# DeltaNet loop in six flows whose TensorE order is written by a planner in the source, with changed inverse and sums of squares

## Chip, cores and metric

The kernel runs on one core of a Trainium2 chip. The metric is the device time of one execution in microseconds; the median of three runs counts.

## The reference

Two encoder layers over x of 1024 tokens x 1024 channels, in f32. Layer 0 is grouped-query attention and a convolutional FFN, layer 1 a bidirectional gated DeltaNet and a convolutional FFN. The change lies in the DeltaNet, cut here to what matters:

```python
qkv, z, ab = split(h @ w_in)                      # 8 heads of q and k, 16 of v and z, 128 wide
qkv = silu(depthwise_conv_centred(qkv, conv_w, conv_b))       # 5 taps along the tokens
q = l2norm(q) * 128 ** -0.5 ; k = l2norm(k)       # each repeated for two v heads
g = -exp(a_log) * softplus(a + dt_bias) ; beta = sigmoid(b)   # per direction
# per direction, chunks of C tokens: decay from cumsum(g), L = (k*beta) k^T * decay below the diagonal
# u, w = (I + L)^-1 [v*beta, k*beta*exp(gc)]
# step: v_new = u - w state ; o = q_dec state + attn v_new ; state = state*g_last + k_dec^T v_new
o = rmsnorm(o_fwd + o_bwd, o_norm) * silu(z)
return o @ w_out
```

## The kernel before

The activations stay in SBUF transposed, channels on partitions. A dense product of f32 data is made from three matmuls of halves in fp32r (high x high, high x low, low x high): `split` (L109, L110) makes the halves, the first on ACT, the second on DVE, and `dense` (L134) issues the matmuls, 128x512 each. A product row (128 output channels, 1024 tokens) is 48 of them, in two PSUM banks of the pool `mm`, which has two such pairs; `sp` has one bank, `ip` one, `cp` two.

The loop runs over eight heads j, each a q and k row and two v and z rows, with two directions d, and each direction over eight chunks of 128 tokens:

- `gdn_in` makes the rows of a head in the order k, q, z0, z1, v0, v1. `conv5` convolves a row from PSUM: ACT writes one tap (L443), DVE adds four (L446), ACT applies the silu (L447). z goes through `gate_rows` (L526) to DRAM. The sums of squares of k and q are lane sums, 16 matmuls for each with a column of ones (L159), over squares by ACT (L480); `rstd` takes the power on GpSimd (L153). k is transposed (L521), scaled on DVE (L490) and transposed back (L493), then the grams k k^T and k q^T are made (L503). v is transposed (L521, copied by ACT at L471), and all go to DRAM in `pk`.
- `decay` (L528 to L553) makes for a head and direction the decayed grams: DMA of the gates, DVE (L541), exp on ACT (L543), products on DVE (L548, L549), halves in f16 (L551, L552).
- `inverse` inverts the unit triangular matrices of 16 chunk-heads together: on 32-blocks three series steps and three doubling levels, each adding a base through a matmul with the identity (`plus`, L589 and L590), then levels for 64 and 128, then one residual step (L668 to L678), whose result 2W + rW is summed in PSUM by a matmul with twice the identity (L676) and copied by ACT (L678).
- `chain` runs the chunks of a direction: state times k and q (L706, L707), DVE makes `r` (L710), the inverse times r (L722), ACT copies `y` (L724), kd times y (L728) updates the state on DVE (L732), pr times y (L734) gives o (L738). GpSimd makes `kd` (L699) and scales the state (L702).
- `head_out` squares o on ACT with its accumulator (L750), scales on GpSimd (L757), transposes (L764) and applies z on DVE (L765).
- When the heads are under way, the first half of the output projection (L818) follows in the same pools.

The order of all engines comes from the tile scheduler, a list scheduler that goes by priorities. `ahead(n)` raises the priority of what is issued in it; in the loop of `gdn`:

```python
with self.ahead(4):
    ah, al, prs = self.decay(j, d, *grams[j], dp)
    ws = self.inverse(d, ah, al, dp)
with self.ahead(2):
    self.chain(j, d, ws, prs, o, dp)
```

The normalisation of k and q has `ahead(2, 1100)`; products, grams, the copies of v and `head_out` have none. The scheduler thus puts the dense matmuls of the products between the dependent steps.

## Time and profile before

| | |
|---|---|
| three runs, median | 3501.07 us (3494.42 to 3502.88) |
| the profiled execution, its own time | 3503.66 us |
| its span in the profile | 3501.9 us |
| mean granted clock of TensorE | 0.983 |
| TensorE busy | 3305.3 us, 94% of the span |
| DVE, ACT, GpSimd busy | 2449.4, 1722.5, 959.9 us |

The span is the time between the first and the last instruction of the profiled execution; 1.8 us of its own time lie around it. Busy times of TensorE overlap, since a matmul begins while the one before ends, so its pace is read from the starts in the timeline. Of the span, the loop of the DeltaNet runs from about 1390 to 2664 us.

### The profile page before, as it was taken

What the parts mean: (1) busy time and instruction counts of PE and PEld (TensorE: products, weight loads), DVE (VectorE), ACT (ScalarE), POOL (GpSimd) and SP (SyncE); (2) the same over time, 40 slices, a digit from 0 to 9 for tenths busy, and PEclk for the clock granted to TensorE, in tenths of its full rate; (3) what the DMA queues carried; (4) which work ended last, traced back from release to release, by engine and by line L of the source; (5) the groups of instructions that cost most, each with busy time, mean ns of one, the idle gap of its engine ahead of it and who ended that gap; (6) DMA issues with size and microseconds to landing.
All of it is one profiled execution on the core that took longest, in us unless ns stands there. A gap on an engine that the chain in (4) does not pass through costs nothing. (4 is left out here: it accounts for less than half of the span.)

```text
span 3501.9 us, 54777 instructions
## 1 busy us (share of the span) xinstructions
PE 3305.3 (94%) x20042; PEld 2651.2 (76%) x20042; DVE 2449.4 (70%) x4133; ACT 1722.5 (49%) x3042; POOL 959.9 (27%) x1122
## 2 busy tenths in 40 slices
PE   7999999899999998999999999999898989999998
PEld 6877878677778786777777777777676867777776
DVE  5325886887777866777767677776763878777685
ACT  4224664544544454555555555556542544444443
POOL 1111230444442002122223233222231154444100
PEclk9999999999999999999999999999999989999999
DMA  3331116333324642333242333324255733322653
GB/s 125 105 103 61 33 33 198 114 103 112 103 100 152 213 132 81 100 98 113 85 135 88 114 110 108 104 88 138 84 179 170 231 105 105 109 94 99 201 163 112
DMA packets 249806, 411.23 MB, mean 117 GB/s; under 512 B 25536, under 2 KB 76096, under 8 KB 249536
## 3 DMA queue, kind: packets, MB, share of 16 engines
q1 hardware_dynamic: 249536, 407.72, 37.0%
q8 instruction: 158, 2.59, 0.3%
q14 instruction: 112, 0.92, 0.1%
HBM read 294.77 MB, written 107.61 MB: 115 GB/s over the span
## 5 line engine op out<-in xcount | busy, mean ns | idle before, releaser
L134 PE MATMUL mm<-base,wh 128*128 128x512 f32 x1248 | 480.3, 412 | 12.5 <-DVE r L818 7.4
L109 ACT CAST wh<-w_raw 128x512 fp32r<-128x512 f32 x275 | 169.8, 619 | 310.3 <-PE mm L134 210.2
L110 DVE TENSOR_TENSOR wl<-w_raw,wh 128x512 fp32r<-128x512 f32 x275 | 194.2, 709 | 147.4 <-ACT wh L109 132.7
L134 PE MATMUL mm<-yh,wh 128*128 128x512 f32 x736 | 286.2, 417 | 3.4 <-ACT yh L109 1.5
L134 PE MATMUL mm<-yl,wh 128*128 128x512 f32 x736 | 285.3, 416 | 0.8 <-DVE yl L110 0.5
L134 PE MATMUL mm<-yh,wl 128*128 128x512 f32 x736 | 282.4, 412 | 1.0 <-DVE wl L110 1.0
L153 POOL TENSOR_TENSOR rs<-rs,power 128x8 f32<-128x8 f32 (+3 forms) x30 | 60.9, 2029 | 810.2 <-DVE rs L152 810.2
L134 PEld LDWEIGHTS mm<-base,wh 128*128 128x128 f32 x1248 | 237.5, 190 | 55.9 <-issue 11.9
L134 PE MATMUL mm<-base,wl 128*128 128x512 f32 x624 | 257.3, 412 | 0.0
L699 POOL TENSOR_SCALAR kd<-c,yds 128x128 f32<-128x128 f32 x224 | 95.1, 436 | 560.7 <-PE cp L728 426.9
L109 ACT CAST wh<-s 128x512 fp32r<-128x512 f32 x216 | 134.1, 621 | 222.1 <-PE sp L134 108.8
L109 ACT CAST wh<-a 128x512 fp32r<-128x512 f32 x164 | 101.7, 621 | 261.6 <-PE mm L134 126.6
L134 PE MATMUL sp<-base,wh 128*128 128x512 f32 (+1 forms) x672 | 210.1, 370 | 1.5 <-DVE ub L995 0.9
L446 DVE SCALAR_TENSOR_TENSOR t<-mm,gdn_cw,t 128x1023 f32<-128x1023 f32 (+1 forms) x128 | 163.0, 1275 | 8.0 <-ACT t L443 6.8
L134 PEld LDWEIGHTS mm<-yh,wh 128*128 128x128 f32 x736 | 140.3, 192 | 28.3 <-ACT yh L109 3.2
L110 DVE TENSOR_TENSOR wl<-s,wh 128x512 fp32r<-128x512 f32 x174 | 144.9, 834 | 23.4 <-ACT wh L109 23.0
L134 PEld LDWEIGHTS mm<-yl,wh 128*128 128x128 f32 x736 | 139.9, 190 | 28.0 <-DVE yl L110 2.4
L134 PEld LDWEIGHTS mm<-yh,wl 128*128 128x128 f32 x736 | 140.3, 191 | 25.6 <-DVE wl L110 1.7
L134 PE MATMUL sp<-base,wl 128*128 128x512 f32 (+1 forms) x432 | 157.2, 364 | 1.6 <-DVE wl L110 1.6
L976 POOL TENSOR_TENSOR s<-a,a 128x512 f32<-128x512 f32 x80 | 105.8, 1323 | 158.4 <-DVE s L976 99.6
L134 PEld LDWEIGHTS sp<-base,wh 128*128 128x128 f32 x672 | 126.4, 188 | 24.2 <-ACT wh L109 2.0
L1054 POOL TENSOR_TENSOR t<-t,t 128x512 f32<-128x512 f32 x66 | 102.6, 1555 | 126.4 <-DVE t L1032 124.5
(536 smaller groups left out, 9510.4 us busy)
## 6 DMA issues: line engine op xcount, KB each, us to landing
a<-in_ffn_up_dram SPq DMA_DIRECT2D x160, 256.0 KB, 3.0
c<-pk SPq DMA_DIRECT2D x128, 320.0 KB, 3.0
w_raw<-in_gdn_in_dram SPq DMA_DIRECT2D x100, 256.0 KB, 3.0
g_t<-t SPq DMA_DIRECT2D x88, 256.0 KB, 2.0
raw<-g_t SPq DMA_DIRECT2D x88, 256.0 KB, 2.7
w_raw<-in_gdn_out_dram SPq DMA_DIRECT2D x68, 256.0 KB, 3.9
g<-t SPq DMA_DIRECT2D x66, 256.0 KB, 2.1
raw<-g SPq DMA_DIRECT2D x66, 256.0 KB, 2.9
```

The costliest lines, as they stand in the source:

```text
L109: self.nc.scalar.copy(out=hi, in_=src)
L110: (engine or self.nc.vector).tensor_tensor(out=lo, in0=src, in1=hi.bitcast(F32), op=ALU.subtract)
L134: self.nc.tensor.matmul(acc if one else acc[:, hs], lhsT=a, rhs=y[:, hs], start=(first and not onto and k + t == 0), stop=(last and k == n ...
L153: nc.gpsimd.tensor_tensor(out=r, in0=v, in1=self.power[:, :w], op=ALU.pow)
L446: nc.vector.scalar_tensor_tensor(out=o, in0=a, scalar=c[:, i:i + 1], in1=o, op0=ALU.mult, op1=ALU.add)
L699: nc.gpsimd.tensor_scalar(out=kd[:, e], in0=kn, scalar1=col(self.yds, e), scalar2=1.0, op0=ALU.mult, op1=ALU.mult)
L976: e.tensor_tensor(out=s[i], in0=x, in1=z, op=op)
L1054: sub = lambda out, x, z: nc.gpsimd.tensor_tensor(out=out, in0=x, in1=z, op=ALU.subtract)
```

## The change

The loop over heads becomes six flows, written as generators: `chains`, `inverses`, `prepare` (transposes, normalisation, grams, copies of v), `decays`, `heads_out` and `products`; the first half of the output projection becomes the end of `products` (`first_out`). A flow yields after some TensorE work the time of that work and the time until its result is there, both as numbers in the source, or the name of a mark that it waits for. `Weave.run` goes on with the first flow, in the order above, that is ready on its clock. TensorE keeps the order in which the instructions are issued (`manual_schedule`); the other engines are ordered by the scheduler, with the flows' priorities 5, 4, 3, 3, 1, 0.

Rows are made in the order k, q, v0, v1, z0, z1; a convolved row counts as ready 8 us after its product. The weights are fetched and split one half row ahead, at priority 1. For the sums of squares, k is copied transposed (ACT), squared by ACT with its accumulator in pieces of 128x128, and scaled by GpSimd in such pieces; q is transposed for that alone. The inverse has one first step and four levels in place of three and three; the identity lies on the diagonal of its operands, so that the matmuls with the identity go; 2W + rW is made by one DVE instruction from PSUM. Some memsets go, the pools `w` and `pr` have eight buffers in place of six, and a chain step writes kd times y into the bank of the state's product.

The order on TensorE, near the end of the loop, between the steps of a chain: from the state times q (`st,c`, 128x256) to the inverse times r (`r,w`) and on to `y,kd`. `mm<-` are dense matmuls. Before:

```order
L707 MATMUL cp<-st,c 128x256
L134 MATMUL mm<-yl,wh 128x512
L134 MATMUL mm<-base_27770,wl 128x512
L134 MATMUL mm<-yh,wl 128x512
L722 MATMUL cp<-r_27543,w 128x128 x2
L134 MATMUL mm<-base_27773,wh 128x512
L134 MATMUL mm<-yh,wh 128x512
L134 MATMUL mm<-base_27773,wh 128x512
L728 MATMUL cp<-y,kd 128x128 x2
```

After the change:

```order
L804 MATMUL cp<-st,c 128x256
L489 MATMUL mm<-base_11445,wl 128x512
L489 MATMUL mm<-yh,wl 128x512
L489 MATMUL mm<-base_11448,wh 128x512
L489 MATMUL mm<-yh,wh 128x512
L489 MATMUL mm<-base_11448,wh 128x512
L489 MATMUL mm<-yl,wh 128x512
L822 MATMUL cp<-r_19835,w 128x128 x2
```

Three dense matmuls stood on each of the two stretches of before. Now six stand on the first, and six more follow up to `y,kd`.

The order on DVE, between the four taps (L446) of a convolved row. Before, a v1 row (L110 splits weights, L753 belongs to `head_out`):

```order
L446 SCALAR_TENSOR_TENSOR t_18779<-mm_18718,gdn_cw_11735,t_18779 128x1022
L446 SCALAR_TENSOR_TENSOR t_18779<-mm_18718,gdn_cw_11735,t_18779 128x1023
L110 TENSOR_TENSOR wl_20343<-w_raw_20341,wh_20342 128x512
L446 SCALAR_TENSOR_TENSOR t_18779<-mm_18718,gdn_cw_11735,t_18779 128x1023
L753 TENSOR_TENSOR ss_20228<-ss_20228,rq_16444 128x8
L110 TENSOR_TENSOR wl_20349<-w_raw_20347,wh_20348 128x512
L446 SCALAR_TENSOR_TENSOR t_18779<-mm_18718,gdn_cw_11735,t_18779 128x1022
```

After, the k row of head 2 up to its third tap (L756 is 2W + rW, L838 adds to o, L595 and L606 belong to `decay`, L871 is z times o):

```order
L446 SCALAR_TENSOR_TENSOR t_14767<-mm_14269,gdn_cw_11730,t_14767 128x1022
L756 SCALAR_TENSOR_TENSOR w_14788<-w0_11722,ip_14783 128x512
L838 TENSOR_TENSOR o_13195<-cp_14762,o_13195 128x256
L446 SCALAR_TENSOR_TENSOR t_14767<-mm_14269,gdn_cw_11730,t_14767 128x1023
L606 TENSOR_TENSOR al_14475<-at_14483,ah_14474 128x512
L595 SCALAR_TENSOR_TENSOR pr_14488<-pr_14488,ebias_11850,maskneg_11724 128x128 x2
L756 SCALAR_TENSOR_TENSOR w_14825<-w0_11722,ip_14820 128x512
L595 SCALAR_TENSOR_TENSOR pr_14488<-pr_14488,ebias_11850,maskneg_11724 128x128 x2
L871 SCALAR_TENSOR_TENSOR z_14807<-sp_14809,gdn_gain_11732,z_14807 128x512
L446 SCALAR_TENSOR_TENSOR t_14767<-mm_14269,gdn_cw_11730,t_14767 128x1023
```

Three other instructions stood between the four taps; now nine stand between the first three taps, and after the third nine more (L602, L756, L603, L672 four times, L606, L858) come ahead of the fourth.

The diff, cut to its core:

```diff
@@ -447,53 +447,96 @@
-    def gdn_in(self, j, ys, tmp, dp, begun=None):
+    def products(self, ys, tmp, begun):
+        nc, w, cw = self.nc, self.ap["gdn_in"], self.cw5
+        rows = [(j, n, i) for j in range(8) for n, i in (("k", 8 + j), ("q", j), ("v0", 16 + 2 * j), ("v1", 17 + 2 * j),
+                                                        ("z0", 32 + 2 * j), ("z1", 33 + 2 * j))]
...
+        for p, (j, name, i) in enumerate(rows):
+            if p < 2:
+                acc = begun[p]
+            else:
+                acc = self.big()
+                for h in range(2):
...
+                    for step in self.steps(acc, split[2 * p - 4 + h], ys[4 * h:4 * h + 4], HALVES, h == 0, h == 1):
+                        yield step
+            if name[0] == "z":
+                self.gate_rows(2 * j + int(name[1]), acc, tmp)
+            else:
+                self.rows[j, name] = self.conv5(acc, cw[:, i], tmp)
+                self.weave.mark((name, j), 8.0)
...
+    def steps(self, acc, w, ys, halves, first, last):
...
+                yield 0.23 * len(halves), 0.0
...
+    def prepare(self, tmp, dp):
...
+        for j in range(8):
...
+            def sums(t, tot):
+                for n in range(4):
+                    sq = dp.tile([P, P], F32, name="sq", bufs=1)
+                    nc.scalar.activation(out=sq, in_=t[:, n * P:(n + 1) * P], func=AF.Square, accum_out=tot[:, n:n + 1])
+            yield "k", j
+            kT = self.rows[j, "k"]
+            kn = []
             for h, hs in enumerate(HALVES):
...
-        with self.ahead(2, 1100):
-            tot = self.bank()
-            for i in range(2):
-                for h, hs in enumerate(HALVES):
-                    sq = tmp.tile([P, H2], F32, name="h", bufs=2)
-                    nc.scalar.activation(out=sq, in_=kq[i][:, hs], func=AF.Square)
-                    self.lane_sums(tot[:, i * NC + 4 * h:i * NC + 4 * h + 4], sq)
-            r = self.rstd(tot[:, :2 * NC], 1, dp)
...
+                t = tmp.tile([P, H2], F32, name="h", bufs=2)
+                nc.scalar.copy(out=t, in_=self.transposed(kT[:, hs]))
+                sums(t, ss[0][:, 4 * h:4 * h + 4])
+                kn.append(t)
+                yield 0.44, 1.2
+            r = self.rstd(ss[0], 1, dp)
             for h, hs in enumerate(HALVES):
-                pt = self.transposed(kT[:, hs])
-                kn = tmp.tile([P, H2], F32, name="h", bufs=2)
-                nc.vector.tensor_tensor(out=chunks(kn), in0=chunks(pt), op=ALU.mult,
-                                        in1=r[:, 4 * h:4 * h + 4].unsqueeze(2).broadcast_to([P, 4, P]))
-                put(2, kn, slice(4 * h, 4 * h + 4))
-                nc.scalar.copy(out=kT[:, hs], in_=self.transposed(kn))
+                for n in range(4):
+                    t = kn[h][:, n * P:(n + 1) * P]
+                    nc.gpsimd.tensor_scalar(out=t, in0=t, scalar1=r[:, 4 * h + n:4 * h + n + 1], scalar2=1.0,
+                                            op0=ALU.mult, op1=ALU.mult)
+                put(2, kn[h], slice(4 * h, 4 * h + 4))
+            yield 0.0, 9.0
+            for h, hs in enumerate(HALVES):
+                nc.scalar.copy(out=kT[:, hs], in_=self.transposed(kn[h]))
+                yield 0.44, 1.5
             put(0, kT)
+            yield "q", j
+            qT = self.rows[j, "q"]
             put(1, qT)
-            kks, qks = {}, {}
+            if j > 0:
+                yield "decay", 2 * j - 1
+            kks, qks = self.grams[j] = {}, {}
             for i in (1, 0):
                 kks[i], qks[i] = (dp.tile([P, H2], F32, name=n, bufs=3) for n in ("kks", "qks"))
...
+                    yield 0.9, 1.2
+            self.weave.mark(("gram", j))
+            for h, hs in enumerate(HALVES):
+                sums(self.transposed(qT[:, hs]), ss[1][:, 4 * h:4 * h + 4])
+                yield 0.44, 2.8
+            r = self.rstd(ss[1], 1, dp)
...
+    def decays(self, dp):
+        for n in range(16):
+            if n % 2 == 0:
+                yield "gram", n // 2
+            if n > 1:
+                yield "half", n - 2
+            self.decayed[n] = self.decay(n // 2, n % 2, *self.grams[n // 2], dp)
+            self.weave.mark(("decay", n), 14.0)
+            yield 0.0, 0.0
...
-        def plus(acc, l, r, base):
-            for m in range(16):
-                nc.tensor.matmul(acc[:, m], lhsT=l[:, m], rhs=r[:, m], start=(m == 0), stop=False)
-            nc.tensor.matmul(flat(acc), lhsT=self.ident16, rhs=base, start=False, stop=True)
...
-                nc.vector.tensor_copy(out=ax[q, hs, q], in_=ah[h][q, :, q])
-            nc.vector.tensor_tensor(out=bx[:, hs], in0=ah[h], in1=every(self.mask4)[:, hs], op=ALU.mult)
-        id_all = every(self.id32)
-        for k in range(3):
-            acc = packed()
-            plus(acc, bx, tp, id_all)
+                nc.vector.tensor_tensor(out=t0[q, hs, q], in0=ah[h][q, :, q], in1=every(self.id32)[q, hs], op=ALU.add)
+            nc.vector.tensor_tensor(out=w0[:, hs], in0=t0[:, hs], in1=every(self.mask2)[:, hs], op=ALU.mult)
+        def evacuated(acc):
             tp = small("tp")
             nc.scalar.copy(out=flat(tp), in_=flat(acc))
+            return tp
...
+        acc = packed()
+        mms(acc, w0, every(self.id32))
...
+        for lv in range(4):
+            if lv:
+                wk = dp.tile([P, 16, 32], F16, name="wk", bufs=1)
+                nc.vector.transpose(out=flat(wk), in_=flat(tp))
+                for q in Q32:
+                    nc.vector.tensor_copy(out=w0[q, :, q], in_=wk[q])
             acc = packed()
-            mms(acc, ax, tp)
+            mms(acc, t0, tp)
+            yield 0.45, 3.2 if lv else 1.4
             x = small("x")
             nc.vector.tensor_tensor(out=x, in0=acc, in1=every(self.lvl[:, d, lv]), op=ALU.mult)
             acc = packed()
-            plus(acc, bx, x, flat(tp))
-            tp = small("tp")
-            nc.scalar.copy(out=flat(tp), in_=flat(acc))
+            mms(acc, w0, x)
+            tp = evacuated(acc)
+            yield 0.45, 1.2
...
+            yield 0.67, 1.2
             acc = self.ip.tile([P, 4, P], F32, name="ip")
             for m in ms:
-                nc.tensor.matmul(acc[:, m % 4], lhsT=r[:, m % 4], rhs=w0[:, m], start=(m % 4 == 0), stop=False)
-            nc.tensor.matmul(flat(acc), lhsT=self.twice16, rhs=flat(w0[:, hs]), start=False, stop=True)
-            ws[h] = dp.tile([P, 4, P], F32, name="w", bufs=6)
+                nc.tensor.matmul(acc[:, m % 4], lhsT=r[:, m % 4], rhs=w0[:, m], start=True, stop=True)
+            ws[h] = dp.tile([P, 4, P], F32, name="w", bufs=8)
+            nc.vector.scalar_tensor_tensor(out=flat(ws[h]), in0=flat(w0[:, hs]), scalar=2.0, in1=flat(acc), op0=ALU.mult,
+                                           op1=ALU.add)
+            yield 0.23, 1.2
+    def chains(self, dp):
+        for n in range(16):
+            j, d = n // 2, n % 2
+            yield "inverse", n
+            if d == 0:
+                yield "rows", j
+                self.outs[j] = [dp.tile([P, 4, 2, P], F32, name="o", bufs=3) for _ in range(2)]
+            ws, prs = self.solved.pop(n)
+            for step in self.chain(n, ws, prs, self.outs[j], dp):
+                yield step
+            self.weave.mark(("chain", n), 1.0)
...
+            if t == 4:
+                self.weave.mark(("half", n0))
+                if d == 0 and j:
+                    yield "head", j - 1
...
+                cc = a[:, 0]
+                yield 0.86, 1.0
             else:
                 r = v
+                cc = self.cp.tile([P, 2, P], F32, name="cp")
...
             nc.scalar.copy(out=y, in_=b[:, 0])
+            yield 0.45, 0.95
             if t < NC - 1:
-                cc = self.cp.tile([P, 2, P], F32, name="cp")
...
+    def heads_out(self, dp):
...
+        for j in range(8):
+            od = [self.dram.tile([P, S], F32, name=f"od{2 * j + e}") for e in range(2)]
+            for i in (1, 0):
+                yield ("half" if i else "chain"), 2 * j + 1
...
+                yield 0.0, 16.0
+                for e in range(2):
...
+                    yield 0.44, 1.5
+            self.od += od
+            self.weave.mark(("head", j))
...
-            grams = {0: self.gdn_in(0, ys, tmp, dp, begun)}
-            for j in range(8):
-                if j < 7:
-                    grams[j + 1] = self.gdn_in(j + 1, ys, tmp, dp)
-                if j == 6:
...
-                for d in range(2):
-                    with self.ahead(4):
-                        ah, al, prs = self.decay(j, d, *grams[j], dp)
-                        ws = self.inverse(d, ah, al, dp)
-                    with self.ahead(2):
-                        self.chain(j, d, ws, prs, o, dp)
-                self.head_out(j, o, dp)
-            os = self.split_rows(self.od[:8], oy, [slice(0, S)], lambda: tmp.tile([P, S], F32, name="t"))
...
+            def first_out():
+                yps.close()
+                oy.append(left.enter_context(tc.tile_pool(reuse_waits="tile", name="oy", bufs=KT)))
+                st.append(left.enter_context(tc.tile_pool(reuse_waits="tile", name="st", bufs=1)))
+                yield "head", 3
+                os = self.split_rows(self.od[:8], oy[0], [slice(0, S)], lambda: tmp.tile([P, S], F32, name="t"))
+                yield 0.0, 6.0
...
+            self.first_out = first_out
+            self.weave = Weave(self)
+            for flow, ahead in ((self.chains(dp), 5), (self.inverses(dp), 4), (self.prepare(tmp, dp), 3), (self.decays(dp), 3),
+                                (self.heads_out(dp), 1), (self.products(ys, tmp, begun), 0)):
+                self.weave.add(flow, ahead)
+            with tc.manual_schedule(engines={mybir.EngineType.PE}):
+                self.weave.run()
...
+class Weave:
+    def __init__(self, trunk):
+        self.t, self.flows, self.marks, self.now = trunk, [], {}, 0.0
+    def add(self, flow, ahead):
+        self.flows.append([flow, ahead, 0.0, None])
+    def mark(self, name, after=0.0):
+        self.marks[name] = self.now + after
+    def ready(self, f):
+        if f[3] is None:
+            return f[2]
+        return max(f[2], self.marks[f[3]]) if f[3] in self.marks else float("inf")
+    def run(self):
+        while self.flows:
+            f = next((f for f in self.flows if self.ready(f) <= self.now), None)
+            if f is None:
+                self.now = min(map(self.ready, self.flows))
+                assert self.now < float("inf")
+                continue
+            f[3] = None
+            with self.t.ahead(f[1]):
+                y = next(f[0], None)
+            if y is None:
+                self.flows.remove(f)
+            elif isinstance(y[0], str):
+                f[3] = y
+            else:
+                self.now += y[0]
+                f[2] = self.now + y[1]
```

## Rows read from the trace of the kernel before

**Rows 1.** Windows, loop stage: us; busy of PE, PEld, DVE, ACT, POOL; clock, DMA, GB/s.

```profile
1390.00:2664.00 1274.00, 1209.71 (x10297) 948.03 (x10296) 891.12 (x2015) 685.15 (x1370) 360.83 (x687) 0.99 0.37 111
```

**Rows 2.** Timeline of PE: start us, duration us, engine, line, instructions.

```profile
1911.09 0.38 PE L670 MATMUL ip<-t,nident 128*128 128x512 f16 x1
1911.12 0.58 PE L134 MATMUL mm<-yh,wl 128*128 128x512 f32 x1
1911.54 0.39 PE L134 MATMUL mm<-base,wh 128*128 128x512 f32 x1
1911.77 0.40 PE L134 MATMUL mm<-yh,wh 128*128 128x512 f32 x1
...
1917.57 0.60 PE L764 MATMUL sp<-ident,o 128*128 128x128 f32 x4
1917.93 0.48 PE L134 MATMUL mm<-yh,wh 128*128 128x512 f32 x1
1918.24 0.39 PE L134 MATMUL mm<-base,wh 128*128 128x512 f32 x1
...
2102.01 0.61 PE L734 MATMUL cp<-y,pr 128*128 128x128 f32 x4
2102.46 1.84 PE L159 MATMUL sp<-ones,h 128*128 128x1 f32 x16
```

**Rows 3.** Waits, loop stage: engine, line <- releaser: us in total, times, longest us.

```profile
PEld cp L722 <- DVE r L710: 34.0, 59, 2.2
...
PEld cp L706 <- DVE st L732: 23.3, 37, 1.5
...
PE cp L722 <- DVE r L710: 18.5, 12, 1.9
...
PEld L675 <- ACT r L672: 13.6, 46, 1.1
...
PEld L589 <- DVE bx L605: 9.9, 16, 1.1
...
PEld sp L764 <- POOL o L757: 7.7, 8, 2.6
...
PEld sp L521 <- ACT t L447: 5.5, 10, 1.9
```

**Rows 4.** Groups of DVE by form, loop stage: xcount | busy us, mean ns | idle before.

```profile
L446 DVE SCALAR_TENSOR_TENSOR t<-mm,gdn_cw,t 128x1023 f32<-128x1023 f32 x60 | 76.7, 1278 | 0.9
L541 DVE SCALAR_TENSOR_TENSOR pr<-pr,ebias,maskneg 128x128 f32<-128x128 f32 x256 | 76.7, 360 | 37.6 <-DMA pr<-grow 36.5
...
L548 DVE TENSOR_TENSOR at<-pr,kks 128x512 f32<-128x512 f32 x64 | 44.9, 702 | 11.2 <-ACT pr L543 10.5
...
L765 DVE SCALAR_TENSOR_TENSOR z<-sp,gdn_gain,z 128x512 f32<-128x512 f32 x32 | 23.9, 747 | 35.4 <-PE sp L764 23.6 <-DMA z<-zd 11.1 <-DVE yl L110 0.6
```

**Rows 5.** Groups of ACT by form, loop stage.

```profile
L750 ACT ACTIVATE sq<-o 128x128 f32<-128x128 f32 x128 | 39.9, 312 | 16.4 <-DVE o L738 13.8
...
L443 ACT ACTIVATE t<-mm,gdn_cw 128x1024 f32<-128x1024 f32 x30 | 36.2, 1206 | 1.0 <-PE mm L134 1.0
...
L447 ACT ACTIVATE t<-t 128x1024 f32<-128x1024 f32 x30 | 31.8, 1060 | 7.1 <-DVE t L446 7.0
...
L447 ACT ACT_TABLE_LOAD x15 | 19.2, 1283 | 0.3
```

**Rows 6.** A slower stretch: timeline of PE, then windows (columns as in rows 1).

```profile
2464.13 0.82 PE L722 MATMUL cp<-r,w 128*128 128x128 f32 x4 [1.88 <-DVE r L710]
...
2464.70:2468.10 3.40, 3.40 (x21) 2.85 (x20) 1.24 (x4) 0.37 (x1) 2.20 (x6) 0.50 0.55 173
```

**Rows 7.** Groups of POOL by form, loop stage, then the durations at L699.

```profile
L757 POOL TENSOR_SCALAR o<-o,ro 128x128 f32<-128x128 f32 x128 | 58.8, 481 | 5.5 <-DVE ro L755 5.5
...
L153 POOL TENSOR_TENSOR ro<-ro,power 128x8 f32<-128x8 f32 x16 | 26.8, 1673 | 241.0 <-DVE ro L152 241.0
...
L699 POOL TENSOR_SCALAR kd<-c,yds x224: 367/376/1242, 1459.4 to 2634.8; 128x128 f32<-128x128 f32 x112
```

More of the change, by code (lines that the diff above doesn't have):

```diff
@@ new lines, in steps @@
+    def steps(self, acc, w, ys, halves, first, last):
+        n = len(ys)
+        for k, ((hi, lo), (yh, yl)) in enumerate(zip(w, ys)):
+            for t, (a, y) in enumerate(((hi, yh), (hi, yl), (lo, yh))):
+                for hs in halves:
+                    self.nc.tensor.matmul(acc[:, hs] if len(halves) > 1 else acc, lhsT=a, rhs=y[:, hs],
+                                          start=(first and k + t == 0), stop=(last and k == n - 1 and t == 2))
+                yield 0.23 * len(halves), 0.0
@@ L660, in inverse @@
             nc.scalar.copy(out=w0[a, hs, b], in_=acc[a])
-        ws = {}
+            yield 0.26, 1.8
+        if n > 1:
+            yield "chain", n - 2
         for h in (range(4) if d == 0 else range(3, -1, -1)):
@@ new lines, in gdn @@
+            x = [self.dram.tile([P, S], F32, name=f"x{m}") for m in range(KT)]
+            self.first_out = first_out
[5 more added lines that the diff above has]
+                self.weave.run()
@@ L1352, in upper @@
         return ((row // b) % 2 == 0) & (row // b == col // b - 1)
[L1354 removed]
+    lv = np.stack([np.stack([m(b) | (row == col) for b in (2, 4, 8, 16)], 1) for m in (lower, upper)], 1)
     a["lvl"] = np.ascontiguousarray(lv.astype(f))
```

191 lines of the change are left out of this document (95 added, 96 removed).

## The prediction

> **What bounds the kernel now.** First the busy time by stage, because the change touches only the loop of the DeltaNet layer: from 1390 to 2664 us TensorE is busy 1209.71 of 1274.00 us and no other engine is above 891.12 [rows 1]. So what counts is TensorE's work and what makes it wait. Second, the pace of that work, from one start to the next in TensorE's timeline, because the records overlap [rows 2]. From 1911.54 to 1911.77 a dense 128x512 takes 0.23 us. From 1911.09 to 1911.54 a 128x512 in f16 and a dense one take 0.45, so the f16 one 0.22. Sixteen lane sums take 1.84, 0.115 each. From 1917.57 to 1918.24 four transposes and a dense one take 0.67, so 0.11 for a transpose. From 2102.01 to 2102.46 two f32 128x128 of the chain (four records) take 0.45. Third, TensorE's waits [rows 3]: each is small (at most 2.6 us). The largest are those of the chain for `r` and for the state `st`, which DVE makes. Convolved rows are hardly waited for: ten waits of the transposes' loads at L521, 5.5 us in the whole loop.
>
> **The change, part by part.** TensorE's instructions first; all of them lie on the path, since TensorE is the bound.
>
> A. Removed: 96 matmuls of 128x512 with the identity (six in each of 16 inverses) and 64 with twice the identity, 160 x 0.22 = 35 us; 256 lane sums, 256 x 0.115 = 29 us. Added: 64 transposes of q, 64 x 0.11 = 7 us. The small 128x32 matmuls stay 2304. Sum **-57 us**, from paces alone.
>
> B. The order of the chain. Before, three dense matmuls (0.69 us) stand between a step that makes the operand of the next and that next step; now six (1.38 us) do on both middle stretches, and four after `kd`. The weight loads waited 34.0 + 23.3 = 57 us for `r` and `st`, the matmuls themselves 18.5 for `r` [rows 3]. The 59 waits of L722 have a mean of 0.58 us, under the 0.69 that is added, the longest 2.2, above it. Bounds: 0 (DVE's queue is ordered by priorities as before and may deliver `r` as much later) and -57. I take **-35**, three fifths, nearer to the mean than to the longest.
>
> C. The inverse: four dense matmuls (0.9 us) before, six (1.34 us) now. The waits for `r` at L675 and `bx` were 13.6 + 9.9 = 23.5 us with means of 0.3 and 0.6 [rows 3]. Bounds 0 and -24; **-14**. D. The heads' outputs: 7.7 us at L764 for GpSimd's scaling [rows 3], now put 16 us behind it; bounds 0 and -8, **-5**.
>
> E. The convolved rows, where the change could lose. A row is TensorE's product, ACT's first tap (1.206 us), four taps on DVE (1.278 each, 5.1 in all) and ACT's silu (1.060, with a table load of 1.283 where another table was in use) [rows 4, 5]. Before, the readers of k, q, v0 and v1 came 46.8, 34.2, 21.9 and 12.9 us of TensorE's work after the product, counted in the order at the paces above. Now the plan puts them 8 us behind the product, and the count gives 7.7 to 14.1, mean 9.7, for the 28 rows of heads 1 to 7. And DVE, whose order the scheduler still makes with products last, has other work between the taps: 5.1 to 18.1 us from first to last tap, mean 10.3. An example is the k row shown from DVE's order (head 2). Between its four taps stand four wide instructions that read PSUM (0.747, as L765), four from SBUF (0.70, as L548) and ten narrow ones (0.36, as L541) [rows 4]: 3.0 + 2.8 + 3.6 = 9.4, with the taps 14.5; with first tap and silu 16.8 us. On TensorE there stand 23 dense matmuls (5.3), 36 of 128x128 in f16 (2.0 at a quarter of 0.22 each), three 128x512 (0.7), eight transposes (0.9), and of the chain two 128x256 and four 128x128 in f32, as much as eight 128x128 at 0.225, so 1.8: 10.7 us. It is 6 us short. The same count over the 28 rows leaves 20 short, by 113 us in sum (4 us for the order before). Below, the bound is 4: the plan's 8 us hold only if DVE leaves the taps together. Above, it is 113. The windows also hold chain and inverse steps that wait for DVE themselves, and while TensorE waits for one row DVE works off what stood before the next, so neither end is likely; no row is near either, and I take the middle, **+55**.
>
> F. The clock. At 2464.13 L722 had waited 1.88 us; from 2464.70 to 2468.10 the granted clock is 0.50, the level of 1.2 GHz [rows 6]. Such a stretch of 3.4 us costs half, 1.7 us. Twenty waits for rows of 55/20 = 2.75 us would be twenty more such stretches (34 us) if each were one wait without a break; bounds 0 and +34, I take six, **+10**.
>
> G. The start. With v ahead of z the third product is convolved too, and its bank is free only after 1.206 + 5.1 us, not after a plain evacuation, once: **+6**.
>
> Costed at nothing, with their cover. The 64 evacuations by twice-and-add on DVE (0.747 each, 48 us) and k's way over GpSimd (64 scalings for 16 DVE products) bring DVE to some 940 us of 1230: covered as long as TensorE's planned distances hold, and what they cost inside the taps is in E. ACT's squares (128 x 0.312 more for k and q [rows 5], each with a read of its accumulator, against 32 wide ones), 16 more copies and 12 more table loads of 1.283 go to an engine that is busy 685 of 1274 us [rows 1]; the loads ahead of the silu are in E. Fewer memsets free GpSimd. k's normalised form has 10.4 to 12.2 us of TensorE's work as cover; it needs 8 squares (2.5), the power on GpSimd (1.673) and 8 scalings (3.85) [rows 5, 7], 8 us, if nothing else is in the queues.
>
> A rule speaks against that last move. The scalings of the heads' outputs take 481 ns in the mean, those of L699 376 in the median and up to 1242 [rows 7]: GpSimd is sometimes held up. The Trainium skill ("SBUF — State Buffer", section "Who interferes with whom") says why: the two engines share a port pair as an exclusive lock, and a VectorE instruction with two SBUF inputs blocks a GpSimd one that reads SBUF for its whole length. By that rule, with such an instruction ahead of each scaling, the maximum would be the normal case and the sum -16 instead of -40 (rival 4); the trace agrees that it occurs, not that it is normal, as the mean of 481 shows.
>
> **The sum.** -57 - 35 - 14 - 5 + 55 + 10 + 6 = -40 us against the profiled execution of 3503.66 us, whose span is 3501.9: 3463.7. That execution is 2.6 us above the median of the runs, so I give **3461 us** for the median. 0.3% (10.5 us) is about what a measurement of this kernel can tell from no change.
>
> **The rivals.**
> 1. *The rows come late in full* (slower). TensorE stands at the first transpose of 20 of 28 rows, in all 113 us, and the clock falls after more of them (+20): -57 - 54 + 113 + 20 + 6 = +28, so 3529, and 3543 with half a microsecond more per row. For it: products have the lowest priority on DVE, and the count itself. Against it: in the trace before, DVE is 30% idle in the loop. It decides from waits of about 4 us per row over 28 rows. Chance 0.22.
> 2. *The rows are in time* (much faster): E at 4, F at 0: -57 - 54 + 4 + 6 = -101, so 3400; with B to D at their bounds 3365. For it: before, 60 such taps of each shape went by with 5.5 us of wait. Against it: there the cover was 1.3 to 4.8 times as long. Chance 0.17.
> 3. *The two cancel* (no change): rows at 95 us, so 3501. Chance 0.11. That the plan is not kept gives the same: TensorE's order is fixed, but the waits of B to D may only move to whatever engine feeds it, since DVE's order is not planned; with those terms at 0 and the rows at 40, the sum is zero.
> 4. *k's normalised form is late*. If each scaling takes GpSimd's 1242 ns, eight of them are 9.9 us and the way is 14 us against a cover of 11: 3 us for each of 8 heads, +24, so 3485. For it: that maximum; against it: the mean of 481 in the same kind of instruction. (The rule of the Trainium skill above is this rival's reason.) Chance 0.05.
>
> **The numbers.** The forecast has 0.45, with its terms between 3420 and 3490. Faster by over 0.3%: 0.45 + 0.17 + 0.05 = 0.67; within 0.3%: 0.11; slower: 0.22. The range 3392 to 3538 leaves out the far end of rivals 1 and 2, a tenth each.
>
> **What the profile would show.** A: the lines of lane sums and of identity matmuls are gone, and TensorE's matmuls in the loop take some 57 us less at the same paces. B and C: the waits for `r` and `st` fall from 57 to about 20 us. E: in the waits, the transposes and the squares' readers wait for ACT's silu, about 2 us in each row. If these waits are above 100 us in sum, rival 1 is right; if under 10, rival 2. F: stretches at a clock of 0.50 follow the transposes' waits. Rival 4 shows as waits of the second transposes of k for GpSimd. The prediction is wrong in its ground if TensorE's waits lie elsewhere, for instance on weights whose split comes late on DVE.

## The result, and the profile after

The changed kernel takes 3637.77 us (3634.67 to 3643.63), the kernel before 3501.03: a ratio of 1.0396 [1.0377, 1.0415], 137 us slower where 40 less were forecast. The profiled execution took 3643.63 us.

The page of the kernel after, first lines:

```profile
span 3641.8 us, 54329 instructions
## 1 busy us (share of the span) xinstructions
PE 3274.0 (90%) x19690; PEld 2671.0 (73%) x19690; DVE 2478.4 (68%) x4199; ACT 1735.5 (48%) x3209; POOL 925.0 (25%) x1111
...
PEclk9999999999999998999999988998989999999999
```

TensorE is busy 31 us less than before and stands still 171 us more (span less busy time). The windows from the first tap of the layer's first convolution to the last addition of the output's first half, of before and after (columns as in [rows 1]):

```profile
1362.10:2711.40 1349.30, 1270.52 (x10570) 995.45 (x10569) 927.79 (x2067) 711.32 (x1407) 363.85 (x688) 0.99 0.38 113
```

```profile
1359.20:2855.70 1496.50, 1243.92 (x10253) 1017.88 (x10252) 965.08 (x2141) 728.58 (x1581) 336.76 (x685) 0.91 0.34 101
```

The whole loss lies in this stretch: it is 147 us longer, where the spans differ by 140. The waits in it, after (columns as in [rows 3]; what was L521 is L575, L722 is L822, L706 is L803, L675 is L754, L589 is L659, L764 is L870):

```profile
PEld sp L575 <- ACT t L447: 178.6, 21, 14.3
PE sp L575 <- ACT t L447: 172.3, 21, 14.2
...
PEld cp L803 <- DVE st L832: 18.8, 17, 2.7
...
PE mm L489 <- DVE t L446: 16.0, 2, 11.1
...
PEld L754 <- ACT r L750: 14.3, 22, 3.3
...
PEld L659 <- DVE w L673: 11.2, 15, 2.9
...
PE sp L870 <- ACT h L566: 2.8, 5, 0.8
```

The first two rows are the result (the same waits, once of the weight load and once of the matmul): TensorE stood 21 times, 8.2 us in the mean, in front of the transposes of a convolved row, where before ten waits made 5.5 us [rows 3]. The loads' wait for `r` at L822 has fallen from 34.0 to 0.7 us and that for `st` from 23.3 to 18.8.

The longest of the 21 is v0 of head 3. Its way through ACT, DVE and TensorE (timelines: start, duration, engine, instruction, in brackets the idle time before):

```profile
1887.27 1.20 ACT L443 ACTIVATE t<-mm,gdn_cw 128x1024 f32<-128x1024 f32 x1
...
1908.92 1.06 ACT L447 ACTIVATE t<-t 128x1024 f32<-128x1024 f32 x1 [5.08 <-DVE t L446]
```

```profile
1888.49 0.35 DVE L595 SCALAR_TENSOR_TENSOR pr<-pr,ebias,maskneg 128x128 f32<-128x128 f32 x1
1888.75 0.69 DVE L602 TENSOR_TENSOR at<-pr,kks 128x512 f32<-128x512 f32 x1
...
1897.25 0.69 DVE L606 TENSOR_TENSOR al<-at,ah 128x512 f16<-128x512 f32 x1
1897.86 0.68 DVE L673 TENSOR_TENSOR w<-t,mask 128x1024 f16<-128x1024 f16 x1
...
1901.88 1.27 DVE L446 SCALAR_TENSOR_TENSOR t<-mm,gdn_cw,t 128x1022 f32<-128x1022 f32 x1
...
1904.35 1.27 DVE L446 SCALAR_TENSOR_TENSOR t<-mm,gdn_cw,t 128x1023 f32<-128x1023 f32 x1
...
1906.29 2.59 DVE L446 SCALAR_TENSOR_TENSOR t<-mm,gdn_cw,t 128x1023 f32<-128x1023 f32 x2
```

```profile
1895.26 0.61 PE L834 MATMUL cp<-y,pr 128*128 128x128 f32 x4
1910.03 1.11 PE L575 MATMUL sp<-ident,t 128*128 128x128 f32 x4 [14.16 <-ACT t L447]
```

ACT has the first tap done at 1888.5, but DVE's first tap starts at 1901.88: for 13 us DVE works without a break on the decay, the inverse, the chain and others, which have a higher priority. Then four more instructions stand between the taps, and the silu ends at 1909.98. The plan counted with 8 us from the product; it took 23.

This row had the longest wait, but no row kept to 8 us. From the start of ACT's first tap to the end of the silu (starts and ends in the timelines) the 28 rows of heads 1 to 7 took 16.0 us in the mean. In the kernel before the same way took 13.9 us, where 12.9 to 46.8 us of TensorE's work stood behind the product to cover it: the trace of before already had a latency well above the 8 us of the plan.

The granted clock around that wait (windows, columns as in [rows 1]):

```profile
1900.60:1914.30 13.70, 4.28 (x15) 3.60 (x15) 8.92 (x17) 3.54 (x4) 4.46 (x9) 0.50 0.17 43
```

The granted clock was 0.50, the lower of its two levels, in the later part of the wait and for 4 us behind it.

A table by stretch helps to compare the runs. For each profiled execution the time between the first convolution's first tap and the last addition of the output's first half is divided: *work* is the count of recorded matmuls times the median pace of their form in the kernel before at the full clock; what a matmul takes beyond that is *clock*, up to one more pace, in stretches granted 0.50, and *wait* for the rest (the waits of weight loads among it). It is an estimate by the rows' paces, good to some us. Each row is one execution, up to 8 us from its kernel's median; that of before took 3503.66 us, while the medians of this kernel in the sessions of the experiments are 3493 to 3499. So differences to the first row are good to some 10 us.

| kernel | window | work | clock | wait |
|---|---|---|---|---|
| before | 1349 | 1180 | 13 | 156 |
| after | 1497 | 1132 | 59 | 305 |
| after, convolutions first | 1386 | 1131 | 41 | 214 |
| after, convolutions first, no fixed order | 1368 | 1135 | 39 | 194 |
| before, all of the change's arithmetic | 1313 | 1126 | 22 | 164 |
| before, lean inverse (sum on TensorE), squares on ACT | 1297 | 1140 | 14 | 143 |
| before, lean inverse alone | 1359 | 1148 | 40 | 171 |
| before, lean inverse (sum on TensorE) alone | 1378 | 1162 | 42 | 174 |
| before, squares on ACT alone | 1333 | 1160 | 15 | 158 |
| before, 160 more wide matmuls | 1375 | 1215 | 16 | 143 |

After against before: 48 us less work, 46 more of clock, 149 more of waits.

### The profile page after: what moved, and what is told of

It reads as the page before. It is cut to its first block, busy times and chain, and to the rows that moved or that the text cites. A ratio compares the mean times of both kernels' runs of the same rounds, so it can differ in the third digit from the quotient of the medians.

```text
span 3641.8 us, 54329 instructions
## 1 busy us (share of the span) xinstructions
PE 3274.0 (90%) x19690; PEld 2671.0 (73%) x19690; DVE 2478.4 (68%) x4199; ACT 1735.5 (48%) x3209; POOL 925.0 (25%) x1111
## 5 line engine op out<-in xcount | busy, mean ns | idle before, releaser
L489 PE MATMUL mm<-base,wh 128*128 128x512 f32 x864 | 386.9, 448 | 18.4 <-DVE t L446 16.0
L110 DVE TENSOR_TENSOR wl<-w_raw,wh 128x512 fp32r<-128x512 f32 x271 | 192.7, 713 | 207.6 <-ACT wh L109 183.9
L153 POOL TENSOR_TENSOR rs<-rs,power 128x8 f32<-128x8 f32 (+2 forms) x38 | 66.6, 1752 | 863.1 <-DVE rs L152 863.1
L575 PE MATMUL sp<-ident,t 128*128 128x128 f32 x256 | 56.2, 360 | 172.9 <-ACT t L447 172.3
L489 PEld LDWEIGHTS mm<-base,wh 128*128 128x128 f32 x864 | 168.7, 195 | 43.7 <-DVE t L446 11.3
L489 PE MATMUL mm<-base,wl 128*128 128x512 f32 x432 | 197.5, 457 | 0.0
L575 PEld LDWEIGHTS sp<-ident,t 128*128 128x128 f32 x256 | 41.0, 186 | 184.6 <-ACT t L447 178.6
L489 PE MATMUL mm<-yh,wl 128*128 128x512 f32 x432 | 175.2, 406 | 0.0
L489 PE MATMUL mm<-yl,wh 128*128 128x512 f32 x432 | 173.3, 401 | 0.9 <-DVE yl L110 0.9
L489 PE MATMUL mm<-yh,wh 128*128 128x512 f32 x432 | 174.1, 403 | 0.0
L446 DVE SCALAR_TENSOR_TENSOR t<-mm,gdn_cw,t 128x1023 f32<-128x1023 f32 (+1 forms) x128 | 163.0, 1276 | 7.7 <-ACT t L443 6.6
L110 DVE TENSOR_TENSOR wl<-s,wh 128x512 fp32r<-128x512 f32 x174 | 145.1, 835 | 24.7 <-ACT wh L109 24.2
L1395 POOL TENSOR_SCALAR p<-p,m 128x1024 f32<-128x1024 f32 x60 | 68.2, 1138 | 233.7 <-DVE m L1394 171.0
```

The costliest lines, as they stand in the source:

```text
L110: (engine or self.nc.vector).tensor_tensor(out=lo, in0=src, in1=hi.bitcast(F32), op=ALU.subtract)
L153: nc.gpsimd.tensor_tensor(out=r, in0=v, in1=self.power[:, :w], op=ALU.pow)
L446: nc.vector.scalar_tensor_tensor(out=o, in0=a, scalar=c[:, i:i + 1], in1=o, op0=ALU.mult, op1=ALU.add)
L489: self.nc.tensor.matmul(acc[:, hs] if len(halves) > 1 else acc, lhsT=a, rhs=y[:, hs], start=(first and k + t == 0), stop=(last and k == n ...
L575: self.nc.tensor.transpose(out=pt[:, n * P:(n + 1) * P], in_=t[:, n * P:(n + 1) * P], identity=self.ident)
L1395: nc.gpsimd.tensor_scalar(out=p, in0=p, scalar1=m[:, 3:4], scalar2=1.0, op0=ALU.mult, op1=ALU.mult)
```

## Experiments

Times are medians; ratios are to the kernel before in the same session, with their interval. The kernel before itself had medians from 3493 to 3501 in the sessions, so a difference between runs of two sessions is given by the times and, where it matters, by the ratios.

**Convolutions first on ACT and DVE.** `ahead(6)` is above the priority of every flow.

```diff
-                self.rows[j, name] = self.conv5(acc, cw[:, i], tmp)
+                with self.ahead(6):
+                    self.rows[j, name] = self.conv5(acc, cw[:, i], tmp)
```

> The changed kernel with the convolutions' instructions at the highest priority on ACT and DVE; TensorE's order is the same. Theory (the rows come late because DVE puts the taps behind its other work): TensorE's waits for the silu at L576 fall from 180 us to under 30, the 11 us wait at the start goes, the clock recovers to about 0.98, and the time falls by 150 to 200 us, to 3440 to 3490, below the kernel before. Rival (DVE has no room left: what is taken from the taps is given back by r, st and the inverse): the waits move to the chain and the inverse, and the time stays above 3560.

Measured 3529.88 us, 1.0093 [1.0076, 1.0110], between the two ranges. TensorE's order is that of the change, so 108 of the 137 us (106 by the ratios) came from when ACT and DVE do the convolutions. The way from ACT's first tap to the end of the silu fell from 16.0 to 9.7 us in the mean. The waits now (of this kernel, whose lines stand one further):

```profile
PE sp L871 <- POOL o L863: 38.8, 20, 11.8
...
PE ip L660 <- DVE w L674: 25.2, 18, 4.0
PE cp L823 <- DVE r L808: 17.9, 27, 1.0
...
PEld sp L576 <- ACT t L447: 2.7, 2, 1.9
```

The wait for the silu fell from 179 to 3 us. But the rival has its part too: GpSimd's scaling, the inverse's first operand and `r` are now late, with the taps ahead of them on DVE, and the kernel stays above the one before.

**A later mark for the rows.**

```diff
-                self.weave.mark((name, j), 8.0)
+                self.weave.mark((name, j), 12.0)
```

> The changed kernel with one number changed: a convolved row counts as ready 12 us behind its product in place of 8. Theory (rows late on DVE): cover grows by 4 us for 28 rows, most of it against waits of 8 us in the mean, so 60 to 100 us less, 3540 to 3580. Rival (the waits follow the row wherever it is placed, since DVE's order moves along): within 30 us of the change, 3610 to 3650.

Measured 3600.11 us, 1.0299 [1.0284, 1.0314]: 38 us less (34 by the ratios), between the two ranges and nearer to the rival. The waits for the silu fell only from 172 to 132 us:

```profile
PE sp L575 <- ACT t L447: 132.2, 17, 15.3
```

So 4 us more for each of 28 rows gave 40 us. The rows moved along in part: their mean way rose from 16.0 to 18.1 us.

**No fixed order on TensorE.**

```diff
-            with tc.manual_schedule(engines={mybir.EngineType.PE}):
-                self.weave.run()
+            self.weave.run()
```

> The changed kernel without the fixed order on TensorE: the scheduler orders TensorE too, with the flows' priorities, work and buffers as in the change. Theory (the loss lies in the planned distances against DVE's order): the scheduler gives the readers of rows more distance, the waits for the silu fall under 60 us and the time to about 3450 to 3530. Rival (the loss lies in the added DVE, ACT and GpSimd work): it stays above 3580.

Measured 3525.23 us, 1.0081 [1.0066, 1.0096], within the theory's range. The scheduler keeps the rows in time, and 113 us of the loss go (110 by the ratios); the kernel is still 0.8% above before.

```profile
PEld sp L575 <- ACT t L447: 2.4, 6, 0.6
```

The rows themselves are no faster here: their mean way is 19.5 us, against 16.0 in the change. So the loss comes from rows and readers that stand too close for DVE's order: more distance, as here, and earlier taps, as with the convolutions first, each take most of it away.

**The leaner inverse alone**, in the kernel before: its `inverse` and `delta_buffers` are replaced by those of the change, without the yields.

```diff
-            plus(acc, bx, x, flat(tp))
+            mms(acc, w0, x)
...
-            nc.tensor.matmul(flat(acc), lhsT=self.twice16, rhs=flat(w0[:, hs]), start=False, stop=True)
-            nc.scalar.copy(out=ws[h], in_=acc)
+            nc.vector.scalar_tensor_tensor(out=flat(ws[h]), in0=flat(w0[:, hs]), scalar=2.0, in1=flat(acc), op0=ALU.mult,
+                                           op1=ALU.add)
```

> The kernel before with the leaner inverse alone (no matmuls with the identity or twice the identity, 2W + rW on DVE, one first step and four levels). Theory: TensorE's work falls by 160 x 0.22 = 35 us and nothing new is waited for, so 3460 to 3475 (25 to 40 us less than before). Rival (DVE's 48 us more make r and st late): no gain or a loss, 3495 to 3530.

Measured 3499.44 us, 1.0014 [1.0003, 1.0024]: no gain, in the rival's range. In the table 32 us of work are gone, and 27 of clock and 15 of waits have come.

**More work on TensorE in the same place**, the mirror of it.

```diff
-            nc.tensor.matmul(flat(acc), lhsT=self.ident16, rhs=base, start=False, stop=True)
+            for k in range(2):
+                nc.tensor.matmul(flat(acc), lhsT=self.half16, rhs=base, start=False, stop=(k == 1))
...
-            nc.tensor.matmul(flat(acc), lhsT=self.twice16, rhs=flat(w0[:, hs]), start=False, stop=True)
+            for k in range(2):
+                nc.tensor.matmul(flat(acc), lhsT=self.ident16, rhs=flat(w0[:, hs]), start=False, stop=(k == 1))
```

> The kernel before with each matmul with the identity done twice with half the identity, and that with twice the identity done as two with the identity: 160 more matmuls of 128x512 in f16, 35 us of TensorE's work, in the place where the change takes 160 away; nothing else. Theory (what a wide matmul adds there is partly given back by waits and by the clock, which fell where the leaner inverse left small matmuls alone): less than half of it is seen, 3495 to 3512, and the time at a clock of 0.50 in the loop falls below the 38 us of before. Rival (TensorE's work is the bound at full price): 3525 to 3535.

Measured 3530.41 us, 1.0118 [1.0101, 1.0135]: 38 us more for 35 us of work (26 in the table, whose execution was the fastest of this kernel's). The rival is right: what is added to TensorE here costs its full price, and the pace in term A holds. So what the leaner inverse saved was lost elsewhere.

**The leaner inverse with its sum on TensorE** (the matmul with twice the identity and ACT's copy stay; the rest as in the leaner inverse alone):

```diff
-            plus(acc, bx, x, flat(tp))
+            mms(acc, w0, x)
```

> The kernel before with the leaner inverse but 2W + rW as before, summed on TensorE by twice the identity and copied by ACT: TensorE loses 96 x 0.22 = 21 us, DVE gains nothing. Theory (in the leaner inverse alone the saving went into DVE's 48 us more and their waits): 3470 to 3480, 15 to 21 us less than before. Rival (it went into the clock, which falls after stretches of small matmuls that the wide ones no longer break up): within 8 us of before, and the time at a clock of 0.50 in the loop stays near 110 us, against 38 before.

Measured 3526.42 us, 1.0099 [1.0082, 1.0116]: slower by 34 us with 21 us less work, outside both ranges. It is not DVE's load, which is near that of before. The rival's mechanism is there: the table has 29 us more of clock, and 18 of waits. A stretch of its timeline of TensorE, and the window that follows:

```profile
1650.69 0.95 PE L159 MATMUL sp<-ones,h 128*128 128x1 f32 x8
1651.50 0.47 PE L134 MATMUL mm<-base,wh 128*128 128x512 f32 x1
1651.91 0.88 PE L632 MATMUL ip<-tp,ah 32*32 32x32 f16 x32
1652.72 0.71 PE L729 MATMUL cp<-y,pr 128*128 128x128 f32 x4
1653.27 0.95 PE L159 MATMUL sp<-ones,h 128*128 128x1 f32 x8
```

```profile
1654.20:1661.00 6.80, 6.80 (x55) 4.81 (x55) 3.55 (x10) 2.58 (x5) 2.92 (x1) 0.50 0.41 157
```

TensorE did not wait there at all. It ran 32 matmuls of 32x32 and 16 of one column (lane sums) with few wide ones between, and then the granted clock was 0.50 for 6.8 us. Nine of the 21 stretches at 0.50 in the window come right behind such 32x32 matmuls of the inverse; of the ten of before none does. In three of the nine no wait stands ahead, and there lane sums stand beside the 32x32 matmuls; in the other six TensorE had also waited, about 1 to 1.7 us, so there the two can't be told apart.

**Sums of squares by ACT and k's scaling by GpSimd alone**, in the kernel before:

```diff
-                    nc.scalar.activation(out=sq, in_=kq[i][:, hs], func=AF.Square)
-                    self.lane_sums(tot[:, i * NC + 4 * h:i * NC + 4 * h + 4], sq)
+                nc.scalar.copy(out=t, in_=self.transposed(kT[:, hs]))
+                sums(t, ss[0][:, 4 * h:4 * h + 4])
...
+                    nc.gpsimd.tensor_scalar(out=t, in0=t, scalar1=r[:, 4 * h + n:4 * h + n + 1], scalar2=1.0,
+                                            op0=ALU.mult, op1=ALU.mult)
```

> The kernel before with the sums of squares by ACT's accumulator, k's scaling by GpSimd and the transposes of q, as in the change, and nothing else of it; the scheduler orders all engines. TensorE's work falls by 22 us (256 lane sums at 0.115 less 64 transposes at 0.11). Theory (saved work is given back as in the leaner inverse alone, where 32 us less work met 27 us of clock and 15 of waits): within 10 us of before, 3485 to 3505. Rival (it pays in full, since lane sums keep TensorE's array nearly idle and their going helps the clock): 3465 to 3480.

Measured 3487.93 us, 0.9991 [0.9979, 1.0002]: no difference that can be told, as the theory had it, for 22 us less of term A's work. The clock is no better without the lane sums, 15 us against 13 in the table. (The profiled execution was 16 us shorter in the window than that of before; the other runs do not bear that out.)

**Both parts**: the leaner inverse with its sum on TensorE, and the squares, in the kernel before (the two edits above together).

> The kernel before with the parts that take work from TensorE and put little on DVE: the inverse without the matmuls with the identity, and the sums of squares by ACT with k's scaling on GpSimd. TensorE's work falls by 21 + 22 = 43 us. Theory (the parts are sound, the planned order is what loses): 3455 to 3475, below before by 20 to 40 us. Rival (what is saved is given back to waits and the clock): 3480 to 3500.

Measured 3442.12 us, 0.9858 [0.9843, 0.9872]: 51 us faster than before, where one part alone lost 34 and the other gave 5. It is below the theory's range, and the fastest version found. (The 5 us of one part alone are not clear of noise.) The table has 40 us less work, clock as before and 13 us less waiting. None of its nine stretches at 0.50 comes behind the 32x32 matmuls. What a part is worth thus depends on the rest. Why is open: the scheduler makes another order of the whole, but the lane sums, which stood beside the 32x32 matmuls ahead of three of the stretches, are gone as well, and the two were not varied apart.

**Both parts, chain ahead of the inverse.**

```diff
-                    with self.ahead(2):
+                    with self.ahead(5):
                         self.chain(j, d, ws, prs, o, dp)
```

> The same two parts in the kernel before, and the chain's priority raised above that of decay and inverse, as the change has it. Theory (r and st are waited for because DVE puts the inverse ahead of the chain, 41 us in the kernel before): 15 to 30 us less than with the two parts alone. Rival (the inverse then comes late and the chain waits for it): no gain, or up to 40 us more.

Measured 3449.62 us, 0.9876 [0.9862, 0.9891]: no gain, the rival.

**All of the change's arithmetic, nothing of its order**: the leaner inverse as in the change and the squares, in the kernel before.

> The kernel before with all of the change's arithmetic (the leaner inverse with 2W + rW on DVE, the sums of squares by ACT, k's scaling on GpSimd) and nothing of its order: the loop, the priorities and the buffers are those of before. Against the same without 2W + rW on DVE (3442): TensorE has 14 us less, DVE 48 us more. Theory (what the change loses against that version lies in its planned order and priorities, not in its arithmetic): 3425 to 3460. Rival (DVE's 48 us are what the change loses): 3480 to 3530.

Measured 3464.16 us, 0.9902 [0.9883, 0.9920], 4 us above the theory's range and well under the rival's. The arithmetic is a gain of 35 us, and 174 us of the change's 3638 lie in the rest of it: order, priorities and buffers. The sum on DVE instead of TensorE costs some 15 us against both parts, by the two ratios (0.9902 against 0.9858 of 3495).

**v ahead of z** on top of that.

```diff
-        z(0)
-        z(1)
         for e in range(2):
             i = 16 + 2 * j + e
             natural(self.conv5(proj(i), cw[:, i], tmp), 3 + e)
+        z(0)
+        z(1)
```

> All of the change's arithmetic in the kernel before (3464), and of its order one thing: the rows of v are made ahead of those of z. Theory (the order of rows matters at the start alone, +6 us in the prediction): 3460 to 3475. Rival (v's rows then come closer to their readers and further from the next product, and the order of rows is a main cause): above 3490.

Measured 3472.03 us, 0.9940 [0.9919, 0.9961], 8 us more, by the ratios 13. The order of rows is a small cause, where the scheduler orders TensorE.

**No fixed order, convolutions first** (the two edits together).

> The changed kernel without the fixed order on TensorE and with the convolutions at the highest priority. With the fixed order the priority gave 108 us (3530), without it the change stands at 3525, its arithmetic alone at 3464. Theory (the fixed order costs what is left, since its distances are constants): 3465 to 3490. Rival (the flows' priorities, the order of rows and the place of the output's first half cost it, whoever orders TensorE): 3510 to 3540.

Measured 3508.93 us, 1.0043 [1.0026, 1.0059], 1 us under the rival's range. The fixed order costs about 20 us beyond its late rows; the other 45 to 50 us above the arithmetic alone lie in what surrounds it, as the rival had it. Where it lies is not shown. 293 dense matmuls come behind the chain's last step, against 176 in the run of the arithmetic alone, 117 x 0.23 = 27 us that cover nothing in the loop. But with v ahead of z, 286 stand there too, and that run lost 8 to 13 us: at most a part of the 45 to 50 is explained by it.

**Convolutions first, the sum back on TensorE.**

```diff
+            nc.tensor.matmul(flat(acc), lhsT=self.twice16, rhs=flat(w0[:, hs]), start=False, stop=True)
...
-            nc.vector.scalar_tensor_tensor(out=flat(ws[h]), in0=flat(w0[:, hs]), scalar=2.0, in1=flat(acc), op0=ALU.mult,
-                                           op1=ALU.add)
+            nc.scalar.copy(out=ws[h], in_=acc)
```

> The changed kernel with the convolutions at the highest priority, and 2W + rW again summed by a matmul with twice the identity and copied by ACT: 14 us more on TensorE, 48 us less on DVE. Theory (with the rows in time, DVE's remaining load is what r, the inverse and the heads' outputs wait for): 15 to 40 us less than with the priority alone, 3490 to 3515. Rival (these waits come from the planned distances, not from DVE's load): 10 to 20 us more, 3540 to 3550.

Measured 3538.44 us, 1.0139 [1.0123, 1.0154], just under the rival's range: 9 us more than with the priority alone (16 by the ratios) for 14 us more of TensorE's work, so 48 us less on DVE brought little. In the planned order DVE's total load is not what is waited for. That DVE's order is what counts fits this, but is not shown by it.

**Convolutions first, two later marks.**

```diff
-                yield 0.0, 16.0
+                yield 0.0, 26.0
...
-            self.weave.mark(("decay", n), 14.0)
+            self.weave.mark(("decay", n), 19.0)
```

> The changed kernel with the convolutions at the highest priority, and two planned latencies longer: the heads' outputs 26 us in place of 16, the decay 19 in place of 14. Theory (the 39 us of waits for GpSimd's scaling and 25 for the first operand of the inverse are planned distances that are too short): both waits fall under 15 us in sum and the time by 30 to 50 us, 3480 to 3500. Rival (what DVE and GpSimd deliver later moves along with the plan): the waits reappear at other readers, 3520 to 3540.

Measured 3520.22 us, 1.0086 [1.0065, 1.0107]: 10 us less than with the priority alone, by the ratios 2, the rival. The wait for GpSimd's scaling did go, but others stand there. The third row lies behind the loop, at the start of the output's second half, so part of what the loop gained was lost behind it:

```profile
PE cp L823 <- DVE r L808: 20.2, 31, 1.1
...
PE ip L660 <- DVE x L695: 18.9, 7, 4.0
...
PE sp L134 <- DVE yl L110: 14.0, 1, 14.0
PE sp L547 <- DVE kks L549: 10.7, 3, 7.9
```

## Why the prediction was wrong

- **A, -57**: as work the term holds. The traces have 352 matmul records less, just those that A takes and adds, and at the paces of before the work in the stretch fell by 48 us, since 36 dense matmuls (8 us) that lay behind it now lie in it. Adding matmuls of that kind cost their full price. As time it holds in part: the arithmetic alone gained 35 us, and parts of it alone gained nothing or lost 34, so "all of them lie on the path" was too simple. That 3464 is near the 3461 given for the whole is chance.
- **B, -35**: the loads' waits for `r` and `st` went from 57 to 19.5 us, the 20 of the text.
- **C, -14**: the same two rows of the inverse make 14.3 + 11.2 = 25.5 us, 23.5 before. Nothing was gained. What used up the longer distance was not traced. (Six dense matmuls are 1.38 us, as in B, not 1.34; nothing hangs on it.)
- **D, -5**: the 7.7 us for GpSimd are gone, 2.8 for ACT have come. Right.
- **E, +55**: this is the step that failed. The waits are 172 us, above the bound of 113 that was called the upper one, and rival 1's own. The count took DVE's work from the first tap to the last and let it begin when ACT was done. For v0 of head 3 that count gave 6.8 us from first to last tap against a cover of 8.6; with first tap and silu it was 0.5 us short. The wait was 14.2, since 13 us of other work stood on DVE ahead of the first tap. Over the 28 rows of heads 1 to 7 the part that was counted is right, 9.7 us in the mean from the first tap to the end of the last, where the text had 10.3. The part that was put at nothing is the queue ahead of the first tap: DVE began it 4.3 us in the mean behind ACT's start, though it could follow after 1.2, which makes 87 us in 28 rows (in nine of all 32 rows it began over 4 us behind). Halving the sum because "DVE works off what stood before the next" then took a bound for too high that was too low.
- **F, +10**: 46 us of clock, not 10. The time at 0.50 in the stretch rose from 38 to 259 us: with waits of 8 us in the mean, 22 of its 29 stretches at 0.50 are 6.8 to 13.7 us long and one 23.9, where nine of the ten of before are 3.4.
- **G, +6**: the waits at the start, for DVE's taps to free a bank, are 16.0 us in two, against 4.0 in one before. The longer was 11.1 us, as v0's second tap came 19 us behind its first.
- Of the rivals the first was right in side and in that the rows come late; its price, 3529, was 109 us short, mainly by E and F. The price for "the rows are in time" (3400) was wrong too: with them in time the kernel takes 3530, since the waits moved to GpSimd's scaling, the inverse and `r`.
- Rival 4 was wrong, and what the Trainium skill's rule ("SBUF — State Buffer", section "Who interferes with whom") tells of cost next to nothing here: k's scalings have a median of 378 ns (the row below, of L526 after), and TensorE's matmuls waited 0.9 us for them, once. That was for the one scaling of 4386 ns, and the trace agrees with the rule there: DVE ran 18 instructions with two SBUF inputs (L595) without a break beside it.

```profile
L526 POOL TENSOR_SCALAR h<-h,rs x64: 368/378/4386, 1391.5 to 2555.6; 128x128 f32<-128x128 f32 x64
```

The sum by these readings: -48 of work, +46 of clock, and of waits +173 for the rows (178.6 against 5.5 of the loads), +12 at the start, -38 for `r` and `st`, +2 and -5: 142, where the spans differ by 140.

## What to carry to other kernels

Where one engine's order is written by hand with assumed latencies and the others are ordered by priorities, the latency of a step holds the backlog of the queue that it enters, also ahead of its first instruction, and not only the sum of its instructions: count from the end of the producer to the consumer, over everything that the queue holds, and compare the number in the plan with what the trace before shows for the same step (8 us against 13.9 here). Work taken off the bounding engine need not pay in full; try parts together as well as alone, since here one part lost 34 us, another made no clear difference, and both gave 51.

## What was not expected of the hardware

The granted clock fell to 0.50 not only behind waits but also behind stretches in which TensorE never stood still. In the run of the leaner inverse with its sum on TensorE this came three times where it had run 32x32 matmuls and one-column lane sums with few wide matmuls between: 6.8 us from 1654.20 is the one shown. The kernel before has one such stretch too, of 3.4 us, behind 16 lane sums without 32x32 matmuls (windows, columns as in [rows 1]):

```profile
1969.74:1973.15 3.41, 3.41 (x27) 2.60 (x26) 0.33 (x2) 0.82 (x3) 2.71 (x1) 0.50 0.34 101
```

In that run of the leaner inverse 126 us of the window were at 0.50, behind waits and without, in the faster one with both parts 41, and the difference in clock, 28 us, is a third of the 81 us between their windows.
